# GpSimd's tables, turns and low parts move to VectorE, decays and the softmax's division to ScalarE

## The chip, the core and the metric

The kernel runs on one core of one Trainium2 chip. The core has a matmul engine (TensorE, in the profile PE; its weight loads are PEld), VectorE (DVE), ScalarE (ACT), GpSimd (POOL) and SyncE (SP), which issues the DMAs here. The engines run side by side, each works through a queue of its own in order, and semaphores hold an instruction back until what it needs is there. The metric is the device time of one execution in microseconds (us); lower is better.

## What is computed

A decoder of two layers on one sequence of 256 tokens of width 1024, all in float32. In each layer a token mixer runs beside a cross-attention with 4 heads into 256 memory tokens; one projection feeds both, one output projection takes both. A SwiGLU feed-forward part with 2816 hidden units follows. The token mixer of layer 0 is a diagonal complex state-space mixer (48 groups of 16 channels with 64 states) with a gated output; that of layer 1 is causal attention with 12 heads and ALiBi, which with 256 tokens is one block.

```python
h = rmsnorm(x, mix_norm_g[i])
proj = h @ w_in                                  # token mixer's inputs and the memory's queries
tok = s5_mixer(...) if i == 0 else moba(...)
x = x + concat([tok, memory_attention(q, mem_k, mem_v)]) @ w_out[i]
x = x + swiglu(rmsnorm(x, ffn_norm_g[i]))
# moba, one head:  softmax(q @ k.T / 8 - slope * dist, causal) @ v
```

The slopes of the 12 heads are 2^(-8(n+1)/12).

## The kernel before

Activations lie with their features on the 128 partitions and the 256 tokens along the row. Most weights are used as a sum of two reduced-precision float32 parts: `split_hi` (line 138) writes the high part `whi` of a raw 128x1024 tile, `split_lo` (line 155) subtracts it from the raw tile and writes the low part `wlo`, and `mm3` (line 185) makes three matmuls of the parts (lines 192 to 194). The raw tiles come in by SP's DMAs through a ring of buffers, one tile for some 24 matmuls, and `weights` (line 173) splits one or two tiles ahead of the one in use. A two-letter code per tile says who splits it: the first letter the engine of the high part (a: ScalarE), the second that of the low part (v: VectorE, g: GpSimd). The codes stand in `ENGINES0` for the six tiles of the gate weights of layer 0 (four of them g) and in `ENGINES1` for the 28 tiles of layer 1's mixer (15 of them g). All other tiles are av; the first tiles of layer 0 are not split.

Each mixer is a hand-written list of steps, `ORDER0` and `ORDER1`, called one after the other. The framework takes this order as a priority and lays out each engine's queue with its own estimates of durations, so that independent steps interleave; buffers that are not free yet hold a step back too.

Steps of layer 0 that matter here, for six units b of eight groups each: `s5_ab` (line 575: two products tA and tB of the input matrices with powers of the decay, in two halves each, and their sum AB), `s5_wo` (line 591: the same for the output, tA, tB and wo, and the angles rc), `s5_rot` (line 619: sines, and the decay spread along the row into `dec`), `s5_scan` (line 679: the recurrence into Z), `s5_turn` (line 693: Z turned back, two products rs and rc) and `s5_y` (line 698: the output's matmuls, lines 704 to 706). One of the two products of each pair was GpSimd's, as were `dec` and the small diagonal `dm` (line 557).

Steps of one attention head, in both layers: scores `s` (a matmul into PSUM), exponential `x` (`h_exp`, line 354), division `n` (`h_norm`, line 373: reciprocal of the sum, then the scaling of p in two blocks, line 378), transposes `t` on the matmul engine, split `h`, values `p` and output `o`. In layer 1 a step `a` (line 955) ahead of the scores has GpSimd write -slope * dist into a table `sb`; VectorE then adds the scores and finds the row's maximum in one pass (line 364), negates the maximum (line 366), and ScalarE takes the exponential. `qe` and `ke` (lines 938 and 941) evict queries and keys from PSUM with the norm's factor (line 307) and split them (lines 272 and 273). `v_evac` (line 292) does so for values.

Of the kernel before, what the change touches and what calls it, by code (L numbers as in the profile page):

```python
# [76 lines left out]
ORDER1 = """
q0 rc a4 v0a v0b rr q1 mq0 mq1 s0 s1 x0 kp0 n0 x1 ve0 a5 t0 n1 h0 s2 x2 a6 qp0 t1 s3 x3 h1 p0 qe0 n2 kp1 ke0
o0 n3 p1 a7 t2 h2 s4 x4 qp2 p2 s5 t3 h3 o1 qp1 a8 n4 qe1 t4 ke1 p3 kp2 x5 s6 s7 x6 h4 qp3 p4 qe2 n5 o2 a9 t5
v1a ke2 qe3 x7 n6 v1b h5 ve1 p5 t6 s8 x8 n7 s9 o3 t7 a10 kp3 a11 x9 h6 h7 o4 p6 n8 t8 qp4 o5 o6 qe4 n9 a12 h8  # L80
ke3 a13 p7 s10 s11 x10 v2a p8 o7 t9 o8 h9 n10 a14 x11 kp4 p9 t10 h10 n11 v2b p10 o9 ke4 t11 h11 ve2 s12 s13
kp5 p11 x12 qp5 x13 n12 n13 qe5 o10 o11 t12 ke5 a15 s14 x14 s15 t13 x15 h12 p12 n14 o12 w0 h13 p13 t14 n15 t15
h14 h15 p14 o13 o14 w1 p15 o15 w2 r0 r1 r2 w3 w4 w5 w6 w7 r3 r4 r5 r6 r7
""".split()
ENGINES1 = """
ag ag ag ag av ag ag ag ag ag ag ag av av av av ag av av av av av ag ag ag av av av
# [3 lines left out]
class Trunk:  # L90
# [29 lines left out]
    def plan(self, name, idx, shape, eng="av"):  # L120

        self.chunks.append((name, idx, shape, eng))

    def load_w(self, n=1, parts=1, between=None):
        for _ in range(n):
            if self.n_load < self.stop:
                name, idx, (a, b), eng = self.chunks[self.n_load]
# [8 lines left out]
                self.loaded.append((raw, b, eng))  # L136

    def split_hi(self):
        nc = self.nc
# [4 lines left out]
        raw, b, eng = self.loaded.pop(0)
        if eng == "":
            self.half.append((raw, None, b, eng))
            return
# [1 line left out]
        if eng[0] == "a":
            nc.scalar.activation(out=hi, in_=raw, func=AF.Copy)  # L150
        else:
            nc.gpsimd.tensor_scalar(hi, raw, 1.0, 0.0, op0=ALU.mult, op1=ALU.add)
        self.half.append((raw, hi, b, eng))

    def split_lo(self):
        if not self.half:
            self.split_hi()
        if not self.half:
            return
        raw, hi, b, eng = self.half.pop(0)  # L160
# [7 lines left out]
        e.tensor_sub(out=lo, in0=raw, in1=f32(hi))  # L168
# [133 lines left out]
    def qk_evac(self, pool, ps, r, nm, bufs, keep=False):  # L302
# [4 lines left out]
        self.nc.vector.tensor_mul(t, ps, r)  # L307
# [46 lines left out]
    def h_exp(self, h):  # L354
        nc, v = self.nc, self.nc.vector
        nm = self.small.tile([P, 2], F32, tag="nm", name="nm")
        if h.slope is None:
            src = h.s
            v.tensor_reduce(nm, src.rearrange("p (a b) -> p a b", a=2), axis=AX.X, op=ALU.max, negate=True)
        else:  # L360
            src = h.sb
# [4 lines left out]
            v.tensor_scalar_mul(nm, mx, -1.0)
        h.sm = self.small.tile([P, 2], F32, tag="sm", name="sm")
        h.p = self.tmp.tile([P, 512], F32, tag="p", name="p")
        for i, c in h.blocks:
            nc.scalar.activation(out=h.p[:, c], in_=src[:, c], func=AF.Exp, bias=nm[:, i:i + 1],  # L370
                                 accum_out=h.sm[:, i:i + 1])

    def h_norm(self, h):
# [3 lines left out]
        for i, c in h.blocks:  # L377
            v.tensor_scalar_mul(h.p[:, c], h.p[:, c], ri[:, i:i + 1])  # L378
# [168 lines left out]
    def s5_buffers(self):  # L547
# [27 lines left out]
    def s5_ab(self, b):  # L575

        v, g = self.nc.vector, self.nc.gpsimd
# [4 lines left out]
        for gg in range(2):  # L582
# [5 lines left out]
            g.tensor_mul(at(m2, gg), be(u.b[1]), co(self.PI))  # L588
        v.tensor_add(u.AB, m1, m2)

    def s5_wo(self, b):

        v, g, con = self.nc.vector, self.nc.gpsimd, self.con
# [5 lines left out]
        g.tensor_mul(gic(m1), ce(u.c[0]), cw(self.WR))  # L599
# [93 lines left out]
    def s5_turn(self, b):  # L693
        u = self.unit[b]
        self.nc.gpsimd.tensor_mul(u.rs, u.z, u.rs)
# [214 lines left out]

    def mixers1(self, pool, xs, sums, cat, order):
# [426 lines left out]
```

## Time and profile before

| what | us |
|---|---|
| median of 3 runs (646.88 to 649.87) | 647.16 |
| the profiled execution's own time | 649.4 |
| its span, first to last instruction | 647.6 |
| PE busy in the span | 615.9 |
| DVE busy in the span | 462.0 |
| ACT busy in the span | 364.0 |
| POOL busy in the span | 94.0 |

The span is what the profile's views divide up; 1.8 us of the execution lie outside it. In a row of a group of instructions stand the line, the engine, the operation, what it writes and reads, the shapes, the count; then busy time in us and the mean of one in ns; then the idle time of the engine just before them and what ended it. A row in order of time begins with the start and the duration in us. A row of a stretch has its two ends, its length, then busy us and count of PE, PEld, DVE, ACT and POOL, the granted clock of the matmul engine (1.00 is full), the share of the DMA engines and GB/s. A row of waits names who waited, for whom, the total in us, how often, and the longest.

### The profile page before, as it was taken

To read this page: it belongs to the slowest core of one execution; us is meant where nothing else is said; L and a number is where in the kernel's file an instruction comes from. 1 tells how busy PE (TensorE), PEld (TensorE's weight loads), DVE (VectorE), ACT (ScalarE), POOL (GpSimd) and SP (SyncE) were. 2 spreads that over 40 slices of the span, in tenths; PEclk is the share of its full clock that TensorE was granted. 3 is DMA by queue.
4 is the path that set the end of the run, shared out by engine and by line. 5 is a ranking of instruction groups with operands and counts; after the bars stand their busy time and mean duration, and the time that the engine had idled before them with its cause. 6 is when DMAs were issued, how large, how long until landed. Compare 5 with 4: busy or idle time off the path is not lost. (4 is left out here: it accounts for less than half of the span.)

```text
span 647.6 us, 12327 instructions
## 1 busy us (share of the span) xinstructions
PE 615.9 (95%) x4808; PEld 585.3 (90%) x4808; DVE 462.0 (71%) x858; ACT 364.0 (56%) x651; POOL 94.0 (15%) x76
## 2 busy tenths in 40 slices
PE   6998889899999999999999999989999999999995
PEld 6877769789999999999999899979999999998884
DVE  7979767679766666666646999978776666664444
ACT  7584826668555555554444758746655555553333
POOL 2435531110000000000036522211000000000001
PEclk9999979899999999999999999979999999999998
DMA  7564231445655565556665334425555655555511
GB/s 216 173 192 117 66 97 50 155 172 185 206 194 192 194 191 193 190 189 182 203 196 184 124 106 156 131 97 167 194 193 192 194 193 194 193 177 181 187 55 66
DMA packets 35578, 105.82 MB, mean 163 GB/s; under 512 B 4032, under 2 KB 9280, under 8 KB 35520
## 3 DMA queue, kind: packets, MB, share of 16 engines
q1 hardware_dynamic: 35520, 105.03, 50.3%
q8 instruction: 38, 0.62, 0.4%
q14 instruction: 20, 0.16, 0.1%
HBM read 102.40 MB, written 1.05 MB: 160 GB/s over the span
## 5 line engine op out<-in xcount | busy, mean ns | idle before, releaser
L150 ACT ACTIVATE whi<-raw 128x1024 fp32r<-128x1024 f32 (+2 forms) x176 | 183.3, 1043 | 151.9 <-PE mm L193 105.6
L168 DVE TENSOR_TENSOR wlo<-raw,whi 128x1024 fp32r<-128x1024 f32 (+1 forms) x157 | 190.0, 1210 | 49.2 <-PE mm L1119 28.3
L168 POOL TENSOR_TENSOR wlo<-raw,whi 128x1024 fp32r<-128x1024 f32 (+2 forms) x19 | 44.8, 2363 | 240.7 <-PE mm L194 208.6
L1057 DVE TENSOR_TENSOR gu<-mm,rr 128x512 f32<-128x512 f32 x44 | 30.4, 692 | 51.4 <-PE mm L194 50.7
L192 PE MATMUL mm<-hh,whi 128*128 128x256 f32 x176 | 48.6, 276 | 0.0
L193 PE MATMUL mm<-hl,whi 128*128 128x256 f32 x176 | 48.6, 276 | 0.0
L194 PE MATMUL mm<-hh,wlo 128*128 128x256 f32 x176 | 48.6, 276 | 0.0
L272 ACT ACTIVATE hh<-ev 128x256 fp32r<-128x256 f32 x44 | 18.3, 419 | 36.7 <-DVE ev L1049 36.7
L192 PEld LDWEIGHTS mm<-hh,whi 128*128 128x128 f32 x176 | 33.0, 188 | 0.0
L193 PEld LDWEIGHTS mm<-hl,whi 128*128 128x128 f32 x176 | 33.0, 188 | 0.0
L194 PEld LDWEIGHTS mm<-hh,wlo 128*128 128x128 f32 x176 | 33.0, 188 | 0.0
L273 DVE TENSOR_TENSOR hl<-ev,hh 128x256 fp32r<-128x256 f32 x44 | 18.7, 425 | 19.7 <-ACT hh L272 19.6
L1146 POOL TENSOR_TENSOR o<-xt,gf 128x256 f32<-128x256 f32 (+1 forms) x3 | 2.8, 921 | 196.7 <-issue 193.3
L192 PE MATMUL mm<-xg0h,whi 128*128 128x256 f32 x102 | 29.8, 292 | 0.0
L193 PE MATMUL mm<-xg7l,whi 128*128 128x256 f32 x102 | 28.4, 278 | 1.1 <-DVE xg7l L268 1.1
L192 PE MATMUL mm<-xg7h,whi 128*128 128x256 f32 x102 | 28.3, 277 | 0.0
L193 PE MATMUL mm<-xg0l,whi 128*128 128x256 f32 x102 | 28.2, 277 | 0.0
L192 PE MATMUL mm<-xg1h,whi 128*128 128x256 f32 x102 | 28.2, 277 | 0.0
L194 PE MATMUL mm<-xg0h,wlo 128*128 128x256 f32 x102 | 28.2, 277 | 0.0
L194 PE MATMUL mm<-xg1h,wlo 128*128 128x256 f32 x102 | 28.2, 277 | 0.0
L193 PE MATMUL mm<-xg1l,whi 128*128 128x256 f32 x102 | 28.2, 276 | 0.0
L192 PE MATMUL mm<-xg2h,whi 128*128 128x256 f32 x102 | 28.2, 276 | 0.0
(429 smaller groups left out, 2188.8 us busy)
## 6 DMA issues: line engine op xcount, KB each, us to landing
raw<-in_w_gu SPq DMA_DIRECT2D x88, 512.0 KB, 3.7
raw<-in_w_down SPq DMA_DIRECT2D x30, 512.0 KB, 3.3
raw<-in_w_qkv SPq DMA_DIRECT2D x18, 512.0 KB, 3.4
raw<-in_w_out SPq DMA_DIRECT2D x16, 512.0 KB, 3.3
raw<-in_w_down SPq DMA_DIRECT2D x16, 448.0 KB, 3.2
raw<-in_w_u SPq DMA_DIRECT2D x5, 512.0 KB, 4.9
raw<-in_w_q SPq DMA_DIRECT2D x4, 512.0 KB, 4.0
wx<-wo SPq DMA_DIRECT2D x12, 128.0 KB, 3.0
```

The lines of the kernel that those rows point to most:

```text
L150: nc.scalar.activation(out=hi, in_=raw, func=AF.Copy)
L168: e.tensor_sub(out=lo, in0=raw, in1=f32(hi))
L192: mm(out, ah, bh, start=(first and i == 0), stop=False)
L193: mm(out, ah, bl, start=False, stop=False)
L194: mm(out, al, bh, start=False, stop=(last and i == n - 1))
L272: self.nc.scalar.activation(out=h, in_=x, func=AF.Copy)
L273: self.nc.vector.tensor_sub(out=l, in0=x, in1=f32(h))
L1057: v.tensor_mul(t, ps, rr.rearrange("p a b -> p (a b)"))
L1146: (nc.gpsimd if i else v).tensor_mul(o[n][:, c], r, gf[:, a:b])
```

## The change

All low parts go to VectorE and the engine codes disappear. In the state-space mixer the second product of each pair (tB, tA, the turn's rs) and `dm` go from GpSimd to VectorE, the spreading of the decays to ScalarE. The two scalings of the softmax's division go from VectorE to ScalarE; the reciprocal stays. The tables of ALiBi are gone: a query is divided by its head's slope when it is evicted, VectorE's pass subtracts the distances themselves from the scores, the slope multiplies the maximum and comes back as the scale of the exponential. The steps `a` leave `ORDER1`; the rest of both lists is as before. GpSimd keeps memsets (twelve small new ones write the slopes' reciprocals into `units`) and three products at the end.

```diff
     def split_lo(self):
...
         lo = self.wlo.tile([P, raw.shape[1]], F32R, tag="wlo", name="wlo")
-        e = self.nc.vector if eng[1] == "v" else self.nc.gpsimd
-        e.tensor_sub(out=lo, in0=raw, in1=f32(hi))
+        self.nc.vector.tensor_sub(out=lo, in0=raw, in1=f32(hi))
...
     def qk_evac(self, pool, ps, r, nm, bufs, keep=False, c=None):
...
-        self.nc.vector.tensor_mul(t, ps, r)
+        if c is None:
+            self.nc.vector.tensor_mul(t, ps, r)
+        else:
+            self.nc.vector.scalar_tensor_tensor(t, ps, c, r, op0=ALU.mult, op1=ALU.mult)
...
             for i, c in h.blocks:
-                v.tensor_tensor_reduce(out=src[:, c], in0=src[:, c], in1=h.s[:, c], scale=1.0, scalar=-3e38,
-                                       op0=ALU.add, op1=ALU.max, accum_out=mx[:, i:i + 1])
-            v.tensor_scalar_mul(nm, mx, -1.0)
+                v.tensor_tensor_reduce(out=src[:, c], in0=h.s[:, c], in1=self.dist[:, c], scale=1.0, scalar=-3e38,
+                                       op0=ALU.subtract, op1=ALU.max, accum_out=mx[:, i:i + 1])
+            v.tensor_scalar_mul(nm, mx, -h.slope)
...
             nc.scalar.activation(out=h.p[:, c], in_=src[:, c], func=AF.Exp, bias=nm[:, i:i + 1],
-                                 accum_out=h.sm[:, i:i + 1])
+                                 scale=h.slope or 1.0, accum_out=h.sm[:, i:i + 1])
...
     def h_norm(self, h):
...
         for i, c in h.blocks:
-            v.tensor_scalar_mul(h.p[:, c], h.p[:, c], ri[:, i:i + 1])
+            nc.scalar.activation(out=h.p[:, c], in_=h.p[:, c], func=AF.Copy, scale=ri[:, i:i + 1])
...
-        nc.gpsimd.tensor_mul(self.dm, ...
+        nc.vector.tensor_mul(self.dm, ...
...
     def s5_ab(self, b):
...
             v.tensor_mul(at(m1, gg), be(u.b[0]), co(self.PR))
-            g.tensor_mul(at(m2, gg), be(u.b[1]), co(self.PI))
+            v.tensor_mul(at(m2, gg), be(u.b[1]), co(self.PI))
...
     def s5_wo(self, b):
...
-        g.tensor_mul(gic(m1), ce(u.c[0]), cw(self.WR))
+        v.tensor_mul(gic(m1), ce(u.c[0]), cw(self.WR))
...
     def s5_rot(self, b):
...
-        nc.gpsimd.tensor_scalar(u.dec.rearrange("p (a b) -> p a b", b=NCH)[:, :, 1:],
-                                self.m4[:, u.G][:, :, None].to_broadcast([P, 2 * UNIT, NCH - 1]), 1.0, 0.0,
-                                op0=ALU.mult, op1=ALU.add)
+        nc.scalar.activation(out=u.dec.rearrange("p (a b) -> p a b", b=NCH)[:, :, 1:],
+                             in_=self.m4[:, u.G][:, :, None].to_broadcast([P, 2 * UNIT, NCH - 1]), func=AF.Copy)
...
     def s5_turn(self, b):
         u = self.unit[b]
-        self.nc.gpsimd.tensor_mul(u.rs, u.z, u.rs)
+        self.nc.vector.tensor_mul(u.rs, u.z, u.rs)
         self.nc.vector.tensor_mul(u.rc, u.z, u.rc)
...
         def qe(p):
-            S.q[p] = self.qk_evac(pool, S.ps[f"qp{p}"], S.r8, "qq", 3, keep=True)
+
+            S.q[p] = self.qk_evac(pool, S.ps[f"qp{p}"], S.r8, "qq", 3, keep=True, c=self.units[:, p:p + 1])
...
-        def alibi(i):
-
-            sb = pool.tile([P, 384], F32, tag="sb", name="sb", bufs=3)
-            self.nc.gpsimd.tensor_scalar(sb, self.dist, -SLOPES[i - MEMH], 1.0, op0=ALU.mult, op1=ALU.mult)
-            S.w[f"sb{i}"] = sb
-
         def scores(i):
             h = head(i)
             if h.slope is not None:
-                h.sb = S.w[f"sb{i}"]
+                h.sb = pool.tile([P, 384], F32, tag="sb", name="sb", bufs=3)
             self.h_scores(h)
...
+        self.units = self.cst.tile([P, HEADS // 2], F32, name="units")
+        for n in range(HEADS):
+            nc.gpsimd.memset(self.units[64 * (n % 2):64 * (n % 2) + 64, n // 2:n // 2 + 1], 1.0 / SLOPES[n])
```

More of the change, by code (lines that the diff above doesn't have):

```diff
@@ L70 @@
 """.split()
-ENGINES0 = """
-ag ag av ag av ag
-""".split()
 ORDER1 = """
[L78 to L86, printed above, removed]
+q0 rc v0a v0b rr q1 mq0 mq1 s0 s1 x0 kp0 n0 x1 ve0 t0 n1 h0 s2 x2 qp0 t1 s3 x3 h1 p0 qe0 n2 kp1 ke0 o0 n3 p1 t2 h2
+s4 x4 qp2 p2 s5 t3 h3 o1 qp1 n4 qe1 t4 ke1 p3 kp2 x5 s6 s7 x6 h4 qp3 p4 qe2 n5 o2 t5 v1a ke2 qe3 x7 n6 v1b h5 ve1 p5
+t6 s8 x8 n7 s9 o3 t7 kp3 x9 h6 h7 o4 p6 n8 t8 qp4 o5 o6 qe4 n9 h8 ke3 p7 s10 s11 x10 v2a p8 o7 t9 o8 h9 n10 x11 kp4
+p9 t10 h10 n11 v2b p10 o9 ke4 t11 h11 ve2 s12 s13 kp5 p11 x12 qp5 x13 n12 n13 qe5 o10 o11 t12 ke5 s14 x14 s15 t13
+x15 h12 p12 n14 o12 w0 h13 p13 t14 n15 t15 h14 h15 p14 o13 o14 w1 p15 o15 w2 r0 r1 r2 w3 w4 w5 w6 w7 r3 r4 r5 r6 r7
 """.split()
@@ L118, in bank, with plan @@
         return getattr(self, "ps_" + kind).tile([P, 512], F32, tag=kind, name=kind)
-    def plan(self, name, idx, shape, eng="av"):
-        self.chunks.append((name, idx, shape, eng))
+    def plan(self, name, idx, shape, split=True):
+        self.chunks.append((name, idx, shape, split))
     def load_w(self, n=1, parts=1, between=None):
@@ L126, in load_w @@
             if self.n_load < self.stop:
[L127 removed]
+                name, idx, (a, b), split = self.chunks[self.n_load]
                 self.n_load += 1
@@ L135, in load_w @@
                         between.pop(0)()
-                self.loaded.append((raw, b, eng))
+                self.loaded.append((raw, b, split))
     def split_hi(self):
@@ L143, in split_hi @@
             return
-        raw, b, eng = self.loaded.pop(0)
-        if eng == "":
-            self.half.append((raw, None, b, eng))
+        raw, b, split = self.loaded.pop(0)
+        if not split:
+            self.half.append((raw, None, b))
             return
         hi = self.whi.tile([P, raw.shape[1]], F32R, tag="whi", name="whi")
[L149 to L153, printed above, removed]
+        nc.scalar.activation(out=hi, in_=raw, func=AF.Copy)
+        self.half.append((raw, hi, b))
     def split_lo(self):
@@ L159, in split_lo @@
             return
-        raw, hi, b, eng = self.half.pop(0)
+        raw, hi, b = self.half.pop(0)
         if hi is None:
@@ L556, in s5_buffers @@
         self.dm = self.s5s.tile([32, NPAIR, 32], F32, name="dm", tag="dm")
-        nc.gpsimd.tensor_mul(self.dm, self.con[0:32, C_E:C_E + 32][:, None, :].to_broadcast([32, NPAIR, 32]),
+        nc.vector.tensor_mul(self.dm, self.con[0:32, C_E:C_E + 32][:, None, :].to_broadcast([32, NPAIR, 32]),
                              self.par[0:32, P_D:P_D + NPAIR][:, :, None].to_broadcast([32, NPAIR, 32]))
@@ L575, in s5_ab @@
     def s5_ab(self, b):
-        v, g = self.nc.vector, self.nc.gpsimd
+        v = self.nc.vector
         u, U = self.unit[b], UNIT
@@ L587, in s5_ab @@
             v.tensor_mul(at(m1, gg), be(u.b[0]), co(self.PR))
-            g.tensor_mul(at(m2, gg), be(u.b[1]), co(self.PI))
+            v.tensor_mul(at(m2, gg), be(u.b[1]), co(self.PI))
         v.tensor_add(u.AB, m1, m2)
     def s5_wo(self, b):
-        v, g, con = self.nc.vector, self.nc.gpsimd, self.con
+        v, con = self.nc.vector, self.con
         u, U = self.unit[b], UNIT
@@ L745, in glu, with plan0 @@
         v.scalar_tensor_tensor(l, w, 0.5, f32(h), op0=ALU.mult, op1=ALU.subtract)
-    def plan0(self, order, engines):
+    def plan0(self, order):
         halfk, full = (KT // 2, T), (KT, P)
@@ L759, in plan0 @@
             at[f"gC{i}"] = ("w_gluC", i, (6, P))
-        engines = iter(engines)
         for name in order:
             if name in at:
-                self.plan(*at[name], next(engines) if name[0] == "g" else "")
+                self.plan(*at[name], name[0] == "g")
     def mixers0(self, memcat, order):
@@ L891, in mixers0, with plan1 @@
         return S.gl
-    def plan1(self, order, engines):
+    def plan1(self, order):
         at = {}
@@ L905, in plan1 @@
             at[f"w{k}"] = ("w_out1", k, (KT, P))
-        engines = iter(engines)
         for name in order:
             if name in at:
-                self.plan(*at[name], next(engines))
+                self.plan(*at[name])
     def mixers1(self, pool, xs, sums, cat, order):
@@ L1163, in run @@
         full, halfk = (KT, P), (KT // 2, T)
-        self.plan0(ORDER0, ENGINES0)
+        self.plan0(ORDER0)
         self.stop = len(self.chunks)
@@ L1180, in run @@
         layer(0)
-        self.plan1(ORDER1, ENGINES1)
+        self.plan1(ORDER1)
         layer(1)
```

3 lines of the change are left out of this document (1 added, 2 removed).

## The prediction, made before the changed kernel ran

> **What bounds the kernel now.** I read the table of busy time by stage first, cut where the work changes: the state-space mixer up to 140 us, the first feed-forward part up to 334, the attention mixer up to 438. Behind it come its output projection and the second feed-forward part.
>
> ```profile
> PE 615.9 (95%) x4808; PEld 585.3 (90%) x4808; DVE 462.0 (71%) x858; ACT 364.0 (56%) x651; POOL 94.0 (15%) x76
> 0.00:20.00 20.00, 15.08 (x66) 13.08 (x67) 16.53 (x90) 11.90 (x27) 5.34 (x15) 0.91 0.71 221
> 20.00:84.00 64.00, 53.78 (x325) 46.21 (x324) 54.99 (x93) 44.25 (x94) 33.11 (x26) 0.97 0.41 125
> 84.00:140.00 56.00, 51.93 (x345) 46.00 (x346) 41.73 (x73) 32.15 (x74) 10.27 (x7) 0.91 0.37 118
> 140.00:334.00 194.00, 194.00 (x1711) 193.95 (x1710) 132.47 (x196) 104.15 (x151) 0.00 (x0) 1.00 0.60 193
> 334.00:438.00 104.00, 99.72 (x811) 94.38 (x810) 84.56 (x215) 66.81 (x155) 40.12 (x26) 0.97 0.41 134
> ```
>
> Behind the stage and its length come PE, PEld, DVE, ACT and POOL in us, then the granted clock. From 140 to 334 the matmul engine has no gap and the clock is 1.00: nothing that other engines do there can shorten it, and POOL does nothing there. POOL works only where PE has gaps: 20 to 84 (10.2 us of them), 84 to 140 (4.1 us, clock 0.91) and 334 to 438 (4.3 us). In two of these DVE is the fullest engine beside PE (55 of 64, 85 of 104). So the change can act on some 19 us of gaps, and on stretches where the clock was halved.
>
> Next the waits of PE, and what DVE and POOL did ahead of two of them:
>
> ```profile
> PE mm L190 <- DVE mv L299: 5.4, 1, 5.4
> PE sc L351 <- DVE qqf L307: 2.8, 1, 2.8
> PE mm L194 <- POOL wlo L168: 0.8, 1, 0.8
> PE sc L706 <- POOL rs L695: 0.6, 1, 0.6
> 418.63 2.94 DVE L378 TENSOR_SCALAR p<-p,ri 128x128 f32<-128x128 f32 x2
> 419.01 2.40 POOL L168 TENSOR_TENSOR wlo<-raw,whi 128x1024 fp32r<-128x1024 f32 x1
> 422.00 0.55 DVE L378 TENSOR_SCALAR p<-p,ri 128x128 f32<-128x128 f32 x2
> 422.28 2.48 POOL L168 TENSOR_TENSOR wlo<-raw,whi 128x1024 fp32r<-128x1024 f32 x1 [0.87 <-PE mm L194]
> 423.03 2.01 DVE L273 TENSOR_TENSOR kkl<-kkf,kkh 128x256 fp32r<-128x256 f32 x1
> L378 DVE TENSOR_SCALAR p<-p,ri x40: 276/348/2561, 99.5 to 432.3; 128x256 f32<-128x256 f32 x28, 128x128 f32<-128x128 f32 x12
> L168 DVE TENSOR_TENSOR wlo<-raw,whi 128x1024 fp32r<-128x1024 f32 x57 | 69.3, 1216 | 2.0 <-PE mm L194 1.1 <-issue 0.9
> L273 DVE TENSOR_TENSOR hl<-ev,hh 128x256 fp32r<-128x256 f32 x22 | 9.4, 425 | 9.9 <-ACT hh L272 9.9
> ```
>
> The DVE instructions that lie beside a POOL instruction end when POOL's ends: the pair at 418.63 takes 2.94 us and ends at 421.6, POOL's at 421.4, while the same pair at 422.00, started ahead of POOL's next, takes 0.55. The subtraction at 423.03 takes 2.01 and ends with POOL's at 425.0; the last two rows are from the stage without POOL and give 425 ns for its shape, and 1216 for the 1024-wide one, for which POOL needs 2.4 us. So POOL's work is not free: DVE stands still for much of it, in the stages where DVE's queue feeds PE. That is what I price.
>
> **The change, part by part.** *State-space stage, 20 to 84.* The rows of DVE in that window, then some rows in order of time:
>
> ```profile
> L587 DVE TENSOR_TENSOR tA<-b,st 128x320 f32<-128x320 f32 x12 | 9.2, 802 | 0.0
> L589 DVE TENSOR_TENSOR AB<-tA,tB 128x640 f32<-128x640 f32 x6 | 7.4, 1238 | 5.7 <-POOL tB L588 4.5 <-issue 1.2
> L600 DVE TENSOR_TENSOR tB<-c,st 128x512 f32<-128x512 f32 x6 | 6.8, 1136 | 0.0
> L601 DVE TENSOR_TENSOR wo<-tA,tB 128x512 f32<-128x512 f32 x6 | 4.1, 676 | 1.0 <-POOL tA L599 1.0
> L696 DVE TENSOR_TENSOR rc<-Z,rc 128x512 f32<-128x512 f32 x3 | 3.5, 1163 | 0.0
> 74.42 0.68 DVE L696 TENSOR_TENSOR rc<-Z,rc 128x512 f32<-128x512 f32 x1
> 75.02 0.69 DVE L603 TENSOR_TENSOR rc<-st,con 128x512 f32<-128x512 f32 x1
> 75.63 0.48 DVE L587 TENSOR_TENSOR tA<-b,st 128x320 f32<-128x320 f32 x1
> 76.03 0.42 DVE L606 TENSOR_SCALAR rs<-rc 128x512 f32<-128x512 f32 x1
> 80.63 2.95 DVE L589 TENSOR_TENSOR AB<-tA,tB 128x640 f32<-128x640 f32 x1 [3.18 <-POOL tB L588]
> 83.50 0.47 DVE L299 SCALAR_TENSOR_TENSOR mv<-mm,rc_mem,mv 128x256 fp32r<-128x256 f32 x1
> ```
>
> Unhindered, the 512-wide product takes 0.68 us and the next starts 0.60 behind it; the 320-wide one 0.48 and 0.40. What goes: 12 x (0.80 - 0.48) + 6 x (1.14 - 0.68) + 3 x (1.16 - 0.68) = 8.0 us of standing, another 2.1 in the one 640-wide sum at 80.63 (0.8 by its size between the 512- and the 1024-wide), and DVE's waits for POOL's products, 4.5 + 1.0. Together 15.6. What comes: 12 tB, 6 tA and 3 turns, 12 x 0.40 + 6 x 0.60 + 3 x 0.60 = 10.2. DVE is rid of 5.4 us net. Of these 3.9 lie on the longest gap of PE, its wait of 5.4 us for the values of the memory (mv): ahead of mv go 3.18 of waiting and 2.1 of standing, and come one turn and two products, 1.4. For the other 1.5 I take their full worth, since PE's other gaps there follow DVE. Term: **-5.4**, between 0 (all of it covered, or DVE's new order puts the two low parts of the gate weights ahead of mv) and -8.
>
> The clock after that gap, and after others (columns as above):
>
> ```profile
> 59.60:62.80 3.20, 0.43 (x5) 0.24 (x3) 3.20 (x5) 0.42 (x1) 1.89 (x2) 1.00 0.41 142
> 63.00:66.40 3.40, 3.40 (x17) 3.40 (x17) 3.40 (x9) 1.70 (x4) 1.40 (x2) 0.51 0.00 0
> 84.00:90.00 6.00, 5.97 (x14) 4.81 (x15) 4.22 (x6) 0.00 (x0) 2.29 (x3) 0.50 0.39 126
> 425.00:431.60 6.60, 5.83 (x28) 5.16 (x29) 4.41 (x20) 3.30 (x11) 0.00 (x0) 0.50 0.47 159
> ```
>
> PE works at half clock for 6 us behind the first gap: 14 instructions, 3.0 us more than at full clock. A gap of 5.4 us shrinks to 1.5; one of 2.8 (from 59.6) was still followed by 3.4 us at half. I take half of the 3.0: **-1.5**, ends 0 and -3.0. The Trainium skill, "TensorE: Matmul & The Clock Gate", section "What's actually happening", has the clock fall after an idle window of about 3.4 us; by that alone the whole 3.0 would go, but the row at 59.6 speaks for a fall after less.
>
> *84 to 140.* PE's two waits for POOL itself, 0.8 and 0.6, go. DVE loses eight divisions and takes three turns and four low parts (768 to 1024 wide, and one of 512), which about cancel. The divisions go to ACT, which is busy for 32 of 56 us there. Term: **-1.4**, between +1 and -3.
>
> *Attention, 334 to 438.* Rows of DVE in that window, and ACT's by form and stage:
>
> ```profile
> L378 DVE TENSOR_SCALAR p<-p,ri 128x256 f32<-128x256 f32 x20 | 14.8, 758 | 0.1
> L378 DVE TENSOR_SCALAR p<-p,ri 128x128 f32<-128x128 f32 x12 | 4.4, 365 | 0.4
> L273 DVE TENSOR_TENSOR kkl<-kkf,kkh 128x256 fp32r<-128x256 f32 x6 | 4.1, 680 | 0.0
> L821 ACT ACTIVATE ms<-xin,par 128x256 f32<-128x256 f32 x8 | 4.0, 502 | 0.0
> L370 ACT ACTIVATE p<-sb,nm 128x128 f32<-128x128 f32 x12 | 4.7, 393 | 3.6 <-DVE nm L366 3.6
> 380.00:400.00 20.00, 19.77 (x171) 18.94 (x170) 18.15 (x59) 16.31 (x41) 4.96 (x6) 1.00 0.47 159
> 400.00:420.00 20.00, 20.00 (x176) 19.49 (x175) 19.18 (x55) 14.75 (x38) 2.49 (x4) 1.00 0.42 133
> ```
>
> DVE loses the 32 divisions, 19.2 us with their standing, and 6 x (0.68 - 0.425) = 1.5 in the key parts: 20.7 at least. It takes 14 low parts at 1.216, 17.0 (the fifteenth of this layer falls behind 438, where it takes 1.2 and frees about as much). The folded slope makes six evictions of queries a three-operand instruction; mv above, of that kind and shape, took 0.47, so it can cost no more than 0.1 each. The tables fall away without a successor: POOL made them, and DVE's pass over the scores now reads the distances in their place. Net DVE is rid of some 3 to 4 us, and more where smaller instructions stood still. The place where it decides is the gap at 422.8: ahead of it 2.94 + 2.01 fall to 0 + 0.425, the pair of 0.55 goes too, and two low parts of 1.216 may come: 5.1 - 2.4 = 2.7 of a wait of 2.8. I take **-2.5** (ends 0 and -2.8), and **-2.0** of the 3.3 us lost at half clock until 431.6 (ends 0 and -3.3), more than half, since this gap closes nearly. For PE's remaining 1.5 us of gaps in this stage **-1.0**. Against it stands ACT: a division of 256 columns costs it about 0.50 (the row of L821, a copy scaled by a column), one of 128 some 0.39, so 20 x 0.50 + 12 x 0.39 = 14.7 us on top of 66.8 of 104. From 380 to 400 ACT is busy for 16.3 of 20, and five heads at 0.89 make 20.8: **+0.8**, ends 0 and +3, as the next 20 us have 5.2 free. Sum of the stage: **-4.7**.
>
> *The rest.* The decays, six copies to ACT, cost about what ACT's 512-wide ones cost, hidden behind a stage in which it is busy for 44 of 64 us; without that cover, less than 1 us each. The diagonal dm and the twelve small memsets come before 20 us, in which PE waits for other things: 0, ends -1 and +1. No DMA is added or moved; SP's queue of weights follows the buffers as before.
>
> **Sum.** -5.4 - 1.5 - 1.4 - 4.7 = -13.0. The profiled execution took 649.4 us for a span of 647.6, so 636.4 by its own time; against the median of the three runs, 647.16, it would be 634.2. I predict **636**.
>
> **Rivals.**
> *The moved work fills the freed place (0.18).* DVE's queue was full for 92% of 380 to 420; if low parts, now in that queue, stand ahead of evictions as POOL's did beside them, only what PE waited for directly goes, 3.9 + 1.4: 649.4 - 5.3 = 644. For it: net DVE is rid of only 3 to 4 us in the attention stage. Against it: a low part held DVE for up to 2.4 us and takes 1.2.
> *ScalarE sets the pace, slower (0.09).* Each head's division waits on ACT for DVE's reciprocal, and the high parts, exponentials and copies behind it wait too. With 8 heads in 380 to 420, ACT's 31.1 us and 8 x 0.89 make 38.2 of 40; each us that a head's reciprocal stands behind DVE work adds 8 us, of which the 1.8 left take little. From about 1 us per head on, it eats the stage's gain; at 2 us it costs 14 in these 40 us. With the 8.3 us of the other stages and no gain in this one that is 649.4 + 14 - 8.3 = 655. Against it: the order puts other work between exponential and division. The Trainium skill, "ScalarE: Activation LUTs", section "Rules for kernel authors", says to multiply on VectorE and not here; the rows agree on the price (348 against 502 ns) but not that VectorE had room.
> *The clock stays full (0.08).* A gate that falls only after some 3.4 us of idling leaves no half-clock stretch at all: -3.0 and -3.3 in place of -1.5 and -2.0, so 649.4 - 15.8 = 633.6. The Trainium skill, in the section on the clock gate named above, states it so; the gap of 2.8 us at 59.6 speaks against it.
> *The change does not act (0.05).* The framework orders every queue anew by its own estimates; the gaps may reappear elsewhere: 648.
>
> **How the numbers follow.** The forecast has 0.60, with a range of its own of 628 to 643. I count as no change what is within 0.5% (643.9 to 650.4), about what a measurement of this kernel can tell. Faster: 0.60 + 0.08 + half of 0.18 = 0.77; same: 0.09 + 0.05 = 0.14; slower: 0.09. Low end 626: all terms at their far ends, -8 - 3 - 3 - 7.6 = -21.6, from the median of 647.16. High end 646: the rival at 644 with 2 us more for ACT. Left out are the 0.09 of the slower rival and the tails.
>
> **What would show it.** Right: DVE's 512-wide products in 20 to 84 all at 0.68, PE's wait for mv under 2 us, the clock at 1.00 in most of 84 to 90 and 425 to 432 (shifted), DVE's busy time in the attention stage 4 to 10 us lower, ACT's some 15 higher. Wrong: PE waits that end on ACT's p, ACT idle until DVE's ri, or a wait for wlo on DVE where POOL's stood.

## The result, and the profile after

| | median us | executions | ratio to the kernel before |
|---|---|---|---|
| before | 648.51 | 4, 646.88 to 650.37 | |
| changed | 628.99 | 4, 628.54 to 629.09 | 0.9697 (95%: 0.9663 to 0.9730) |

The changed kernel is faster by 19.5 us, 3.0%. The forecast was 636, its range 626 to 646: sign and mechanism came out, the size was 1.5 times what was forecast. The profiled execution has a span of 627.3 us against 647.6. The line of busy times on its page:

```profile
PE 607.7 (97%) x4808; PEld 579.3 (92%) x4808; DVE 446.7 (71%) x862; ACT 380.6 (61%) x697; POOL 5.7 (1%) x26
```

POOL's 94 us are gone, yet VectorE, which took most of that work over, is busy for 15 us less. Fixed times no longer cut the work at the same places, so the stages are cut here at five instructions that both kernels have: the first transpose of the state-space mixer, the gate's first matmul, the first matmul of the first feed-forward part, the first matmul that makes the attention mixer's values, and the end of the last low part of its output on VectorE (xg7l). The view of stretches, of the kernel before:

```profile
27.05:99.84 72.79, 62.54 (x371) 53.64 (x371) 58.42 (x98) 45.73 (x101) 31.59 (x25) 0.93 0.40 119
99.84:161.02 61.18, 57.13 (x455) 53.67 (x454) 49.41 (x85) 41.13 (x85) 7.72 (x4) 0.97 0.46 145
161.02:346.28 185.26, 184.73 (x1628) 184.48 (x1627) 120.73 (x172) 96.08 (x135) 9.72 (x4) 1.00 0.60 195
346.28:457.79 111.51, 107.19 (x874) 101.65 (x873) 97.36 (x240) 74.55 (x171) 32.81 (x23) 0.97 0.42 136
```

and of the changed kernel:

```profile
27.20:83.10 55.90, 54.90 (x347) 46.73 (x346) 47.32 (x101) 45.30 (x98) 0.00 (x0) 1.00 0.45 133
83.10:145.52 62.42, 57.43 (x477) 54.60 (x477) 53.36 (x98) 48.68 (x103) 0.00 (x0) 1.00 0.48 154
145.52:329.96 184.44, 184.44 (x1629) 184.38 (x1627) 123.16 (x176) 96.11 (x135) 0.00 (x0) 1.00 0.61 196
329.96:438.13 108.17, 106.08 (x874) 101.49 (x873) 85.73 (x219) 84.86 (x203) 0.00 (x0) 0.98 0.43 140
```

Call the four rows A to D. PE's gaps are the length less PE's busy time. What the throttle (which sets the granted clock) took is counted as half of the time at half clock; that comes in windows of 3.41 us, three in A (1 - 0.93 of 72.8 us, 5.1), one in B and two in D before, and one in D after. Where PE would have waited anyway it took less; and this is the account of two traced executions. The rest is, in A and B, matmul instructions that changed sides of the cut.

| stretch | length | PE's gaps | lost to the clock, at most | rest |
|---|---|---|---|---|
| A, state space | 72.8 to 55.9: -16.9 | 10.3 to 1.0: -9.3 | 5.1 to 0: -5.1 | -2.5 (371 to 347 instructions) |
| B, gate to feed-forward | 61.2 to 62.4: +1.2 | 4.1 to 5.0: +0.9 | 1.7 to 0: -1.7 | +2.0 (455 to 477) |
| C, first feed-forward | 185.3 to 184.4: -0.8 | 0.5 to 0: -0.5 | 0 | -0.3 |
| D, attention | 111.5 to 108.2: -3.3 | 4.3 to 2.1: -2.2 | 3.4 to 1.7: -1.7 | +0.6 |

The stretch behind D gave another 0.6. So the state-space stage with the gate behind it gave 15.7 of the 20.3 us by which the spans differ. Rows of VectorE between 20 and 76 us of the changed kernel:

```profile
L577 DVE TENSOR_TENSOR tA<-b,st 128x320 f32<-128x320 f32 x10 | 4.8, 481 | 0.0
L578 DVE TENSOR_TENSOR tB<-b,st 128x320 f32<-128x320 f32 x10 | 4.8, 480 | 0.0
L590 DVE TENSOR_TENSOR tB<-c,st 128x512 f32<-128x512 f32 x5 | 3.4, 685 | 0.0
L685 DVE TENSOR_TENSOR rc<-Z,rc 128x512 f32<-128x512 f32 x3 | 2.0, 672 | 0.0
```

Each product now takes what the prediction called unhindered: 0.48 for 320 columns (0.80 before), 0.67 to 0.69 for 512 (1.14 and 1.16 before). Two products one after the other (481 + 480 ns) take 0.96 us, where one beside POOL's took 0.80. PE's longest waits of the changed kernel between its first transpose and the end of D, from the view of waits:

```profile
PE sc L341 <- DVE qqf L297: 1.4, 1, 1.4
PE sc L693 <- ACT p L360: 1.1, 1, 1.1
PE sc L693 <- ACT tm L637: 1.0, 1, 1.0
PE mm L181 <- DVE wlo L155: 0.9, 1, 0.9
```

The wait for mv (5.4) is gone, the one for the query (qqf) halved. Of the two that end on ScalarE, both in B, the one for the exponential (p) rose from 0.2 to 1.1; the one for the copy tm was there before (0.9).

### The profile page after: what moved, and what is told of

Same layout as the page of the kernel before. It is cut to its first block, busy times and chain, and to the rows that moved or that the text cites. A ratio compares the mean times of both kernels' runs of the same rounds, so it can differ in the third digit from the quotient of the medians.

```text
span 627.3 us, 12242 instructions
## 1 busy us (share of the span) xinstructions
PE 607.7 (97%) x4808; PEld 579.3 (92%) x4808; DVE 446.7 (71%) x862; ACT 380.6 (61%) x697; POOL 5.7 (1%) x26
## 4 chain that ended last, share of the span: by engine, by line
PE 86%; ACT 6%; DVE 5%; DMA 1%; issue 1%; SPq 0%; ACTq 0%; DVEq 0%
PE mm L179 21%; PE mm L180 21%; PE mm L181 21%; PE mm L177 4%; PE sc L1099 2%; PE sc L1100 2%; PE sc L1101 2%; PE sc L177 1%; DVE wlo L155 1%; PE tp L1101 1%; PE tp L1099 1%; PE tp L1100 1%; PE pv L207 1%; ACT p L360 1%; PE tp L373 1%
## 5 line engine op out<-in xcount | busy, mean ns | idle before, releaser
L155 DVE TENSOR_TENSOR wlo<-raw,whi 128x1024 fp32r<-128x1024 f32 (+2 forms) x176 | 210.6, 1198 | 50.6 <-PE mm L1100 28.3
L180 PE MATMUL mm<-xg2l,whi 128*128 128x256 f32 x102 | 28.3, 277 | 0.0
L179 PE MATMUL mm<-xg5h,whi 128*128 128x256 f32 x102 | 28.2, 277 | 0.0
L179 PE MATMUL mm<-xg4h,whi 128*128 128x256 f32 x102 | 28.2, 277 | 0.0
```

The costliest lines, as they stand in the source:

```text
L155: self.nc.vector.tensor_sub(out=lo, in0=raw, in1=f32(hi))
L179: mm(out, ah, bh, start=(first and i == 0), stop=False)
L180: mm(out, ah, bl, start=False, stop=False)
```

## The experiments

The question was which part of the change carries the gain, by which mechanism, and whether the division belongs to ScalarE. Times are medians; the changed kernel stands at 628.99 in its first set and 628.66 in a second one. The kernel before ran beside every set of experiments, with medians of 648.4, 648.9 and 648.1.

**The products of the state-space mixer.** First back on GpSimd, all else as changed:

```diff
-            v.tensor_mul(at(m2, gg), be(u.b[1]), co(self.PI))
+            self.nc.gpsimd.tensor_mul(at(m2, gg), be(u.b[1]), co(self.PI))
...
-        v.tensor_mul(gic(m1), ce(u.c[0]), cw(self.WR))
+        self.nc.gpsimd.tensor_mul(gic(m1), ce(u.c[0]), cw(self.WR))
...
-        self.nc.vector.tensor_mul(u.rs, u.z, u.rs)
+        self.nc.gpsimd.tensor_mul(u.rs, u.z, u.rs)
```

> The changed kernel with the second product of each pair in the state-space mixer (12 tB, 6 tA, 6 turns) back on GpSimd. Theory A, these products account for most of the gain, since the state-space mixer with its output projection became 15.5 us shorter: 639 to 644 us. Rival B, the gain there came from the low parts of the gate weights, whose subtraction on GpSimd stood beside the 640-wide sum at 80.6 us: 629 to 633 us.

Measured: 633.49 (633.43 to 637.44), ratio 0.9798 (0.9753 to 0.9842): 4.7 us above the changed kernel, between the two expectations. Then these three edits alone, in the kernel before:

> The kernel before with only the 24 products of the state-space mixer on VectorE, all else as before. Theory A: 634 to 640 us. Rival B: 644 to 649 us. If the parts only pay together (VectorE without the relief of the division): slower than 649 us.

Measured: 639.08 (637.22 to 639.47), ratio 0.9863 (0.9826 to 0.9901): 9.3 below before. The rows A and B of the first and A of the second:

```profile
31.19:97.31 66.12, 59.22 (x372) 50.70 (x371) 58.27 (x99) 49.00 (x107) 23.35 (x19) 0.97 0.41 129
97.31:154.22 56.91, 54.77 (x455) 52.15 (x454) 45.10 (x80) 44.11 (x94) 2.82 (x2) 1.00 0.48 155
```

```profile
28.89:91.40 62.51, 58.96 (x371) 51.34 (x371) 53.81 (x105) 46.81 (x102) 7.49 (x6) 0.97 0.42 131
```

With the products back, A is 10.2 us longer (66.1 against 55.9); B is 5.5 shorter, as the instructions that had moved behind the gate stand ahead of it again (372 and 455, as before) and PE's gaps in B are 2.1 in place of 5.0. Alone, the products shorten A by 10.3 of the 16.9. Undone they cost 4.7, alone they bring 9.3: the parts don't add up. (These profiles begin with different starts, 25.5 to 31.2 us to the first transpose, without relation to the edits; so stretches are compared, not ends. The traced execution with the products back is the slowest of its four, 637.44, with the latest start.)

**The low parts.** Nineteen of them back on GpSimd, those that had been there:

```diff
+LOWS0 = list("ggvgvg")
+LOWS1 = list("ggggvgggggggvvvvgvvvvvgggvvv")
...
-        self.nc.vector.tensor_sub(out=lo, in0=raw, in1=f32(hi))
+        e = self.nc.vector if self.lows.pop(0) == "v" else self.nc.gpsimd
+        e.tensor_sub(out=lo, in0=raw, in1=f32(hi))
```

> The changed kernel with the 19 low parts (4 of the gate, 15 of layer 1) back on GpSimd. Theory A: the attention mixer loses its gain of some 4 us and the gate part 1 to 2, 632 to 636 us. Rival B: 639 to 644 us. Rival C, low parts on GpSimd only hurt while VectorE also had the division: under 631 us.

Measured: 632.00 (630.05 to 632.35), ratio 0.9754 (0.9716 to 0.9791): 3.0 above the changed kernel, at the lower end of what was expected. Its rows C and D:

```profile
145.34:330.58 185.24, 184.71 (x1628) 184.46 (x1627) 120.63 (x172) 96.07 (x135) 9.72 (x4) 1.00 0.57 194
330.58:441.04 110.46, 106.37 (x874) 101.68 (x873) 81.18 (x208) 85.29 (x203) 26.40 (x11) 0.97 0.40 138
```

C is at 185.24 again, 0.8 more: the whole gain of C is that of four low parts, which GpSimd makes near its end. D is 2.3 longer, though VectorE has eleven subtractions less to do. A and B together are unchanged (118.4 us against 118.3), so the gate's four cost nothing measurable.

**Standing or work?** What would GpSimd's work cost if nobody needed it? In two kernels it makes a copy of what VectorE makes into a tile that nobody reads: all 24 products, or 768 columns of fifteen low parts in layer 1. In two others it reads one column in the same places and fills more columns than the copy had, so that it is busy about as long almost without reading. The edits of the first pair, for the products:

```diff
+            self.nc.gpsimd.tensor_mul(at(self.new("jk", 1, n), gg), be(u.b[1]), co(self.PI))
...
+        self.nc.gpsimd.tensor_mul(gic(self.new("jw", 1)), ce(u.c[0]), cw(self.WR))
...
+        self.nc.gpsimd.tensor_mul(self.new("jw", 1), u.z, u.rs)
```

```diff
+        self.nc.gpsimd.tensor_scalar(j[:, 0:1], x, 1.0, 0.0, op0=ALU.mult, op1=ALU.add)
+        self.nc.gpsimd.memset(j[:, 0:n], 0.0)
```

> The changed kernel, in which GpSimd also makes the 24 products of the state-space mixer, into tiles that nobody reads; VectorE makes its own. Theory L, GpSimd's reads of SBUF make VectorE's instructions stand still: products of 320 and 512 columns on VectorE again above 0.8 and 1.0 us in the mean, and 636 to 644 us. Rival W, the loss before was the wait for GpSimd's slower results: 629 to 631 us, since nobody waits here.

> As the run with the unread products, but GpSimd only fills a tile with zeros for about as long, behind one read of a single column that ties it to the same moment. Theory L, with the standing tied to GpSimd's reading: VectorE's products stay at 0.48 and 0.68 us, 629 to 631 us. If any GpSimd work beside VectorE does it: 636 to 644 us, as with the unread products.

Measured: 640.02 (638.76 to 642.27), ratio 0.9863 (0.9827 to 0.9899), for the reads, and 629.79 (627.85 to 631.27), ratio 0.9701 (0.9660 to 0.9742), for the fills. Rows A and B of the reads, then A of the fills:

```profile
26.92:90.17 63.25, 56.99 (x348) 47.68 (x347) 60.73 (x109) 46.57 (x100) 25.29 (x17) 0.97 0.40 120
90.17:156.15 65.98, 60.23 (x478) 57.09 (x477) 54.61 (x98) 48.72 (x103) 4.61 (x3) 0.95 0.45 147
```

```profile
27.21:82.91 55.70, 54.89 (x348) 46.77 (x347) 49.69 (x104) 45.31 (x98) 28.79 (x26) 1.00 0.46 138
```

POOL is busy for 25 us of A in the one and 29 in the other; the one is 7.4 us longer than the changed kernel, the other not at all (55.7 against 55.9). From the start to the end of B VectorE runs the same 306 instructions in all three: it is busy for 124.0 us in the changed kernel, 125.7 with the fills and 137.8 with the reads. Of the 11 us that the reads cost in A and B, gaps are 6.0 (6.3 and 5.8 against 1.0 and 5.0) and the clock at most 5.1 (three windows of 3.41 at half, one in A and two in B). VectorE's rows, of the reads and then of the changed kernel:

```profile
L577 DVE TENSOR_TENSOR tA<-b,st 128x320 f32<-128x320 f32 x10 | 6.8, 681 | 0.0
L229 DVE SCALAR_TENSOR_TENSOR rc<-rs_w,rc 128x2 f32<-128x2 f32 x2 | 1.8, 891 | 0.0
```

```profile
L229 DVE SCALAR_TENSOR_TENSOR rc_mem<-rs_w,rc_mem 128x2 f32<-128x2 f32 x3 | 0.4, 149 | 0.0
```

A product of 320 columns rises from 481 to 681 ns on the mean, short of the 0.8 us that was expected, and the 512-wide ones stay at 0.68 against the 1.0 expected. What stands longest for its size is small: an instruction on two columns rises from 149 to 891, as it waits for whatever GpSimd is doing. So the mechanism is VectorE standing still beside reads of GpSimd. No result of GpSimd's is waited for in this kernel. But three turns on VectorE wait until GpSimd has read the rs that they overwrite, 3.5 us in all; that is another cost, and here it can't be taken apart from the standing in the length of A and B. The pair of runs on the low parts, below, has no such wait. GpSimd being busy is nearly free: the fills add 1.7 us to VectorE, on a few single instructions (two that write diag take 1.11 us each in place of 0.28). The Trainium skill, "SBUF — State Buffer", section "Who interferes with whom", has it so: a VectorE instruction with two inputs in SBUF (the on-chip memory that holds the tiles; PSUM holds the matmuls' results) contends with a GpSimd instruction that reads SBUF, not with one that only writes it. Both runs agree with that: the reads made VectorE stand for 13.8 us, and the two-source products beside the fills kept their 0.48 us.

For the low parts the same pair:

```diff
+            self.nc.gpsimd.tensor_sub(out=j, in0=raw[:, 0:768], in1=f32(hi)[:, 0:768])
```

```diff
+            self.nc.gpsimd.tensor_scalar(j[:, 0:1], f32(hi)[:, 0:1], 1.0, 0.0, op0=ALU.mult, op1=ALU.add)
+            for _ in range(2):
+                self.nc.gpsimd.memset(j, 0.0)
```

> The changed kernel, in which GpSimd also subtracts 768 of 1024 columns of the 15 low parts of layer 1 that it had before, into a tile that nobody reads. Theory L: VectorE's instructions beside them stand still for up to 2 us, the attention mixer becomes 2 to 6 us longer, 631 to 635 us. Rival W: 629 to 630 us.

> As the run with the unread low parts, but GpSimd only fills the tile twice with zeros. Theory L with the standing tied to reads: 629 to 630 us. If any GpSimd work does it: 631 to 635 us.

Measured: 639.44 (636.32 to 644.11), ratio 0.9856 (0.9802 to 0.9910), and 630.53 (627.06 to 631.12), ratio 0.9702 (0.9664 to 0.9740). The fills cost 1.5 by the medians, just outside what was expected, and 0.3 in D (108.5 against 108.2) in the traced execution, the fastest of the four. The reads cost 10.5, more than was expected. Their rows D, reads first:

```profile
332.69:448.82 116.13, 108.55 (x874) 102.89 (x873) 96.42 (x219) 85.03 (x203) 21.96 (x11) 0.97 0.38 132
```

```profile
327.60:436.06 108.46, 106.26 (x874) 101.41 (x873) 86.94 (x219) 84.81 (x203) 19.57 (x33) 0.98 0.41 140
```

VectorE has the same 219 instructions in D and is busy for 96.4 us against 86.9: 22 us of GpSimd's reading make VectorE stand for some 9.5, and D 7.7 us longer. That low parts on GpSimd without the copy on VectorE cost only 2.3 in D is then no puzzle: VectorE loses 11 subtractions by it. With the reads PE's wait for the query is back at the 2.8 us of the kernel before. Rows in order of time around it:

```profile
412.25 3.77 POOL L162 TENSOR_TENSOR jk<-raw,whi 128x768 f32<-128x768 f32 x2 [5.25 <-ACT whi L144]
412.46 1.89 DVE L267 TENSOR_TENSOR gl<-otile,gl 128x256 fp32r<-128x256 f32 x1 [0.82 <-ACT gl L266]
414.27 0.47 DVE L304 SCALAR_TENSOR_TENSOR qqf<-mm,units,rr 128x256 f32<-128x256 f32 x1
414.80 0.38 PE L348 MATMUL sc<-kkf,qqf 64*128 64x128 f32 x2 [2.83 <-DVE qqf L304]
```

The subtraction gl, with both inputs in SBUF, takes 1.89 us beside GpSimd's read (0.42 in the changed kernel); the query's eviction behind it, one of whose large inputs lies in PSUM, keeps its 0.47 beside GpSimd's next read. It is late, not slow.

**The division.** One line, the division on VectorE again, timed twice; the second time beside the changed kernel and a version with the division on VectorE in the first layer alone:

```diff
-            nc.scalar.activation(out=h.p[:, c], in_=h.p[:, c], func=AF.Copy, scale=ri[:, i:i + 1])
+            v.tensor_scalar_mul(h.p[:, c], h.p[:, c], ri[:, i:i + 1])
```

> The changed kernel with the softmax's division back on VectorE. If the division on ScalarE gave VectorE room (the prediction's reading): 630 to 633 us. If ScalarE now holds up the matmul engine by it (waits of the matmul engine on ScalarE's p, tm and yh between 84 and 112 us are new): 625 to 628 us.

> The changed kernel unaltered, timed on the same chip as the three that follow: 627 to 631 us. It is the measure for them; nothing is told apart by it alone.

> The softmax's division on VectorE, all else as in the changed kernel, once more. Theory S (in the second attention ScalarE's order is the tighter one: the division takes 0.50 us there against 0.35 on VectorE, and it delays the exp, the high parts and the query chain behind which the clock halves): 624 to 627, at least 1.5 below the changed kernel on this chip, with no stretch of half clock at 400 to 420 us. Rival (the single interval seen so far was a lucky fall of the clock): 627.5 to 631, level with it, and the half clock is back.

> The division on VectorE in the first layer alone, where it lies beside the state-space work. Theory S, with the second attention as the place: 627 to 631, level with the changed kernel, the state-space stage at 55 to 57 us from first transpose to the gate's first matmul. Rival (the gain comes from ScalarE's load in the first layer, which falls by 3 us in the stage): 624.5 to 627.

Measured:

| division on | median | executions | ratio to before |
|---|---|---|---|
| VectorE, first time | 626.46 | 624.83 to 627.04 | 0.9677 (0.9636 to 0.9718) |
| VectorE, again | 626.82 | 624.90 to 628.86 | 0.9672 (0.9638 to 0.9707) |
| ScalarE (changed kernel) again | 628.66 | 628.34 to 629.10 | 0.9705 (0.9677 to 0.9734) |
| VectorE in layer 0 alone | 629.42 | 627.71 to 631.78 | 0.9716 (0.9685 to 0.9748) |

The intervals of the ratios overlap, but nine of the ten executions with the division on VectorE lie below all ten of the changed kernel: it is some 2 us faster. This is the fastest version of the study. The first expectation named the right time for a wrong reason: with the division on VectorE PE's waits on tm and yh in B are longer (1.6 and 0.8 us against 1.0 and 0.6), not gone. Rows D of the second time, then B and D of the version with layer 0 alone:

```profile
332.60:436.94 104.34, 103.67 (x874) 99.37 (x873) 92.96 (x251) 74.27 (x171) 0.00 (x0) 1.00 0.41 145
```

```profile
82.41:146.83 64.42, 58.20 (x477) 54.76 (x477) 55.35 (x106) 47.59 (x97) 0.00 (x0) 1.00 0.45 151
331.27:438.51 107.24, 104.94 (x874) 99.93 (x873) 85.74 (x219) 84.92 (x203) 0.00 (x0) 1.00 0.41 141
```

The gain is in D: 104.3 against 108.2, with 7.2 us more work on VectorE and 10.6 less on ScalarE. In layer 0 it is the other way: B is 64.4 against 62.4, and A and B together are 119.5 to 119.8 us in the three traces with the division on VectorE, against 118.3 and 118.1 in the two of the changed kernel. Part of the gain in D is a half-clock window that the changed kernel has and this one hasn't; the version with layer 0 alone, whose D has its divisions on ScalarE too, hasn't it either, and its D is 107.2: so 2.9 us come without the clock. ScalarE looks like the right place for layer 0's divisions and is the wrong one for layer 1's; a kernel with only the latter on VectorE was not run. Why ScalarE costs in D is seen in the order of time, around the changed kernel's wait for the query (ScalarE's and VectorE's rows, then PE's):

```profile
401.93 1.48 ACT L368 ACTIVATE p<-p,ri 128x128 f32<-128x128 f32 x4
403.44 0.38 ACT L398 ACTIVATE ot<-pv 64x256 f32<-64x256 f32 x1
403.84 0.42 ACT L259 ACTIVATE kkh<-kkf 128x256 fp32r<-128x256 f32 x1
404.17 1.04 ACT L140 ACTIVATE whi<-raw 128x1024 fp32r<-128x1024 f32 x1
405.11 0.40 ACT L259 ACTIVATE gl<-otile 128x256 fp32r<-128x256 f32 x1
405.55 0.42 DVE L260 TENSOR_TENSOR gl<-otile,gl 128x256 fp32r<-128x256 f32 x1 [0.82 <-ACT gl L259]
405.89 0.48 DVE L297 SCALAR_TENSOR_TENSOR qqf<-mm,units,rr 128x256 f32<-128x256 f32 x1
406.42 0.49 PE L341 MATMUL sc<-kkf,qqf 64*128 64x128 f32 x4 [1.38 <-DVE qqf L297]
```

Four blocks of division hold ScalarE for 1.48 us without a break; the eviction ot, the high part kkh, the weights' high part and the copy gl stand behind them. VectorE's next in its queue, gl's low part, waits 0.82 us for that copy, the query's eviction stands behind it, and PE waits 1.38 us for the query. The wait carries VectorE's name; it begins on ScalarE. It is there again (1.4) in the version with layer 0 alone on VectorE, and gone in both traces with all divisions on VectorE.

**The tables.** Back on GpSimd, with the slope in the table instead of in the query, and the steps `a` in the order:

```diff
+            self.nc.gpsimd.tensor_scalar(sb, self.dist, -SLOPES[i - MEMH], 1.0, op0=ALU.mult, op1=ALU.mult)
...
-                v.tensor_tensor_reduce(out=src[:, c], in0=h.s[:, c], in1=self.dist[:, c], scale=1.0, scalar=-3e38,
-                                       op0=ALU.subtract, op1=ALU.max, accum_out=mx[:, i:i + 1])
-            v.tensor_scalar_mul(nm, mx, -h.slope)
+                v.tensor_tensor_reduce(out=src[:, c], in0=src[:, c], in1=h.s[:, c], scale=1.0, scalar=-3e38,
+                                       op0=ALU.add, op1=ALU.max, accum_out=mx[:, i:i + 1])
+            v.tensor_scalar_mul(nm, mx, -1.0)
```

> The ALiBi tables (12 of 0.52 us, one source in SBUF) on GpSimd again, the slopes out of the queries and back in the tables; all else as in the changed kernel. Theory L (what costs is GpSimd reading while VectorE works, in proportion to its time: 6.3 us of tables against 20 us of products that cost 4.5 and 41 us of low parts that cost 3): 0.5 to 1.5 above the changed kernel, 628.5 to 631. Rival (the chain table, sum and maximum is what the second attention gained by): 631.5 to 633.5, the second attention's stage 2 to 4 us longer.

Measured: 627.68 (626.00 to 630.36), ratio 0.9692 (0.9659 to 0.9725). Neither expectation held: the tables cost nothing measurable on GpSimd. Row D, from the slowest of the six executions:

```profile
331.20:439.25 108.05, 106.04 (x874) 101.49 (x873) 86.26 (x219) 84.86 (x203) 8.12 (x12) 0.98 0.41 140
```

Twelve tables keep POOL busy for 8.1 us, VectorE for 0.5 more than without them (86.26 against 85.73), and D is as long as in the changed kernel. So the cost of GpSimd's reads isn't in proportion to their time. The order of time shows what these meet. Ten of the twelve tables take 0.64 us or less, and most of the large instructions of VectorE beside them have an input in PSUM and keep their time (qqf at 371.00 takes 0.42). The other two begin while VectorE subtracts a low part: it keeps its 1.23 and 1.22 us, and the table takes 1.31 and 1.57, so there it is GpSimd that stands. Which of these makes the tables free was not tested by itself.

## Why the prediction was right, and where its sizes were off

**The mechanism** was read rightly from the pairs in the order of time: VectorE stands still beside GpSimd's reads. The copies that nobody reads showed it by itself, those of the low parts without any wait of VectorE for GpSimd. One reading was a little off: kkl at 423.03 doesn't end with POOL's subtraction but 0.28 us behind it (425.04 against 424.76).

**State space, -5.4, and 84 to 140, -1.4.** The two terms are about PE's gaps, 6.8 together; in A and B the gaps fell by 8.4. The split was off: A gave 9.3, B lost 0.9. In A the prediction took the net work that VectorE is rid of, 5.4, with 3.9 of it on mv's wait. What it counted, standing and waits, did go; it left the order of VectorE's queue as it was. The sums of the stretches from 27 us to the end of mv, before and after, and the rows of AB in them:

```profile
sum 58.00, PE 47.75 PEld 41.13 DVE 50.32 ACT 40.30 POOL 29.79; mean PE 47.75 PEld 41.13 DVE 50.32 ACT 40.30 POOL 29.79
L589 DVE TENSOR_TENSOR AB<-tA,tB 128x640 f32<-128x640 f32 x5 | 6.6, 1321 | 4.3 <-POOL tB L588 3.2 <-issue 1.2
```

```profile
sum 47.20, PE 46.20 PEld 39.15 DVE 39.64 ACT 38.18 POOL 0.00; mean PE 46.20 PEld 39.15 DVE 39.64 ACT 38.18 POOL 0.00
L579 DVE TENSOR_TENSOR AB<-tA,tB 128x640 f32<-128x640 f32 x4 | 3.3, 818 | 2.1 <-PE tp L630 2.1
```

VectorE's busy time ahead of mv fell by 10.7 us, and the stretch by 10.8 (58.0 to 47.2): part of it is standing that is gone, and one of five units' products now comes behind mv. In B the waits on POOL went as forecast; the wait on ScalarE's exponential p grew from 0.2 to 1.1, and one of 0.9 for wlo on VectorE came. In the attention ScalarE idles 1.7 us for VectorE's ri. So the signs that the prediction had listed as "wrong" are all there, each of about a microsecond.

**The clock, -1.5. In the two traces this is the term that missed most.** It counted the 6 us at half clock behind mv's gap, took half of them, and gave no credit for the stretches at 63 and 117.6, since "one of 2.8 (from 59.6) was still followed by 3.4 us at half". All of them went: up to 6.8 us in A and B (5.1 and 1.7), 5.3 more than forecast, while the gaps missed theirs by 1.6. Half clock may cost less than it is counted at, where a faster PE would have waited longer. In 25 timed executions of the kernel before the mean granted clock ranges from 0.975 to 0.990. The nine at 0.975 to 0.978 average 649.7 us, the four at 0.990 645.1: 4.6 us between them, where half of the time at half clock makes 8. And those four are still 16 us above the changed kernel, whose clock is 0.991 to 0.993. By this estimate the clock's share of the gain is some 4 to 5 us and not 8.5; those executions have no trace, so how the miss divides between clock and gaps stays open.

The forecast judged by the length of one gap whether the clock would fall. Rows of one window of 3.41 us and the one behind it, in the kernel before, then in the one with layer 0's division on VectorE:

```profile
114.15:117.56 3.41, 1.86 (x12) 1.23 (x10) 3.41 (x6) 2.49 (x7) 1.24 (x1) 1.00 0.48 156
117.56:120.97 3.41, 3.02 (x14) 3.03 (x15) 1.38 (x4) 0.00 (x0) 0.33 (x1) 0.50 0.02 5
```

```profile
404.20:407.61 3.41, 2.16 (x20) 1.92 (x18) 2.05 (x6) 3.36 (x7) 0.00 (x0) 1.00 0.45 154
407.61:411.02 3.41, 3.28 (x24) 2.63 (x25) 3.15 (x12) 1.69 (x6) 0.00 (x0) 1.00 0.31 96
```

The granted clock changes on a fixed raster of 3.41 us (in the kernel before at 62.94, 66.36, 83.42, 90.25, 117.56 and 120.97 us, whole multiples apart). The window at 114.15, in which PE worked for 1.86 us (0.55) with its gaps in pieces, none over 0.93, was followed by half clock; the one with 2.16 (0.63) was not, nor was one with a single gap of 1.78 in another run. So the length of one wait, by which the forecast weighed a gap of 1.5 us against another of 2.8, doesn't decide it. The busy share of a window is a better guide, though no sharp one, as the last section shows. Before, three full-clock windows of A and B had PE busy for 0.55 of their length or less, with half clock behind them; after, the lowest share in A and B is 0.65. That this one stayed at full clock may be luck, since a window of 0.65 in D did not.

**Attention, -4.7.** Measured -3.3: gaps -2.2 against -2.7 forecast (2.5 and 1.0 less the 0.8 for ScalarE), the clock -1.7 against -2.0. VectorE's busy time in D fell by 11.6 (4 to 10 forecast), ScalarE's rose by 10.3 (some 15). The term that was mis-sized is ScalarE's **+0.8**, ends 0 and +3: with the division on VectorE D is 3.8 us shorter: 1.4 by gaps (2.1 to 0.7), 1.7 by the half-clock window, 0.7 within PE's busy time. The price of one division was right; rows of ScalarE between 318 and 420 us:

```profile
L368 ACT ACTIVATE p<-p,ri 128x256 f32<-128x256 f32 x20 | 9.6, 498 | 1.0 <-DVE ri L366 1.0
L368 ACT ACTIVATE p<-p,ri 128x128 f32<-128x128 f32 x12 | 4.7, 395 | 0.7 <-DVE ri L366 0.7
```

0.50 and 0.39 had been taken. What was wrong is to ask how full ScalarE is over 20 us. In the one place that could be followed, what counted is what stands behind a block of divisions when PE's next operand depends on that queue.

**The rivals.** "The moved work fills the freed place" fell: VectorE is less busy in A and D, with more instructions in A. "ScalarE sets the pace" was right that what stands behind a division waits for it, but the wait for the reciprocal, on which its price rested, is small (1.7 us in all), and the price far too large: about 2 us over the whole kernel, not 14 in 40. The rule of the Trainium skill quoted with it, "ScalarE: Activation LUTs", section "Rules for kernel authors", to multiply on VectorE, holds in layer 1 and not in layer 0, by the lengths of D and of A and B above. "The clock stays full" came true in A and B and not in D. "The change does not act" fell.

**The rest, 0,** was -0.8 in C, by four low parts, and -0.6 behind D.

**Left open.** Undone one at a time, the products cost 4.7, the low parts 3.0, the tables nothing measurable, the division less than nothing; the whole is 19.5. The copies suggest why, at 11.0 and 10.5: a part that is moved to GpSimd also takes work off VectorE, and a copy does not. Moving the decays and dm was not undone by itself. With the division, the tables and the folded slopes they are what the version with low parts back has over the one with the products alone, 639.08 to 632.00, some 7 of the 19.5. In their traces D is 110.46 us in both, A is 3.4 shorter and B 0.8 (and the start, which varies by itself, 2.0). So what was gained lies in layer 0: the decays, dm and its divisions. Which of these gave how much isn't settled.

## What to carry to other kernels

An engine that looks free isn't, if its reads stop the one beside it: set the two engines' rows side by side in the order of time, and see whether they end together. Take its reads away where they meet instructions that PE's next operand depends on; where they are short and meet others (the tables) it made no difference here. When gaps of PE close, count the clock as well: it gave up to 8.5 of the 20.3 us between the two traces, and it is read window by window, not gap by gap.

## What the hardware showed unasked

Over the fourteen traces of this study, between 25 and 600 us, all eight full-clock windows of 3.41 us in which PE was busy for 0.47 of the window or less were followed by half clock. Of 31 with 0.48 to 0.69, eight were; above 0.69, none. So these records don't show what decides in that range. In the changed kernel a window with 2.21 us (0.65) was followed by half clock:

```profile
405.22:408.63 3.41, 2.21 (x15) 1.55 (x16) 2.82 (x6) 2.47 (x5) 0.00 (x0) 1.00 0.33 101
408.63:412.04 3.41, 3.41 (x17) 3.41 (x18) 2.25 (x13) 2.12 (x10) 0.00 (x0) 0.50 0.81 298
```

while the 2.16 shown above, in the same part of the work at another phase of the raster, was not. The Trainium skill, "TensorE: Matmul & The Clock Gate", section "What's actually happening", knows the free-running window of 3413 ns, and the rows agree with that; but it has the clock fall after an idle window, where here it fell after windows that were busy for up to 0.69 of their length.
